# A hybrid decoder block on one core: the key's decay to its block's end from a backward scan

## The chip, the core and the metric

The kernel runs on one core of a Trainium2 chip. TensorE multiplies matrices, VectorE (DVE) and ScalarE (ACT) work element by element, GpSimd (POOL) does small side work, and SyncE (SP) issues nearly all DMA transfers. The metric is the device time of one execution in microseconds; the time before is the median of three runs. Each profile shows one execution.

## The reference

The input x has 1024 tokens of 1024 features, in float32. One layer computes

```python
proj = x @ w_in        # -> q, f, i, o_gate, pool_v, gate_a, gate_b
f = lb + (1 - lb) * sigmoid(f_pre);  k = 1 - f;  log_f = log(f)
# S_t = diag(f_t) S_{t-1} + k_t v_t^T,  o_t = S_t^T q_t,  for 8 heads of 128, in blocks of 16 tokens:
G = cumsum(log_f within a block);  G_last = its last value
q_dec = q * exp(G);  k_inv = k * exp(-G);  k_to_end = k * exp(G_last - G)
scores = causal(q_dec @ k_inv^T);  o = scores @ v + q_dec @ state
state = exp(G_last) * state + k_to_end^T @ v
a = (rmsnorm(o) * g * sigmoid(o_gate)) @ w_a
b = (causal_mean_w(pool_v) - pool_v) @ w_pool * pool_scale
x = LN(alpha * x + (sigmoid(gate_a) * a + sigmoid(gate_b) * b) @ w_out)
x = LN(alpha * x + relu(x @ w_up)^2 @ w_down)
```

Three quantities matter here. exp(G) is the product of the forget gates f from the start of a block up to and with a token. exp(-G) is its inverse. exp(G_last - G) is the product of the gates behind a token up to the block's end.

## The kernel before

Every large product is made in a form with seven block products in place of eight, and each operand is split into a high and a low part in a rounded format, so that one float32 product is three matmuls (lines 199 to 201: high by high, high by low, low by high; each 128 x 128 by 128 x 512). The split of a weight (lines 117 and 118) is a cast on ScalarE into `hi` and a subtraction on VectorE into `lo`. There are ten weight tiles (`NW`), so five pairs. `pair` makes two columns of blocks at a time; results leave PSUM by a copy on ScalarE (line 268) or a sum on VectorE (line 272), and functions called `take` do what follows (a sigmoid, for example).

The stages are: the values i (up to about 100 us of the profile); the stage of the recurrence, in which the projections for q, f, the output gate, the pools and the gates run between the recurrences of 8 heads in 2 halves of 512 tokens (about 120 to 560 us); the pooling products and the end of the gates (to about 650 us); w_a and w_out with the merge, the first layer norm, then w_up and w_down and the second layer norm (to the end).

`hgrn(h, u, ...)` is the recurrence of one head h in one half u. Features lie on the 128 partitions and tokens along the free axis. 512 tokens are 32 blocks of 16 (`NB`, `SUB`). Line 808 makes `fd`, the products of the gates from each block's start, with a scan over 256 tokens at a time: the state is at each step the larger of itself and an entry of `starts`, times the gate; `starts` is 1 at a block's first token and 0 elsewhere, and as all products are at most 1, the scan begins anew at each block. Line 810 on ScalarE turns the gates into k = 1 - f in place. Lines 812 to 814 invert all of `fd` (`r`, tile tC) in four pieces of 128. GpSimd copies the 32 block ends of `fd` into `T` (line 816) and makes the small products for 32 and 64 tokens, `p32`, `p64`, `eq`, `ek` and `dec`, from it (to line 835). VectorE multiplies q by `fd` (line 838), makes the key to its block's start, `kc = k * r` (line 840, tile tD), and the key to its block's end, `kr = kc * T` (line 842, tile tE).

The score is made over pairs of blocks of 16. For each pair there is a reference point in its middle: the end of the even block. The keys of an even block are taken at its end (line 843 copies them from `kr` over `kc` on ScalarE), and the queries of an even block are divided by the block's whole decay (line 846, with `r` at the block's last token). The keys of an odd block stay at its start, and so do its queries (line 845). Then lines 850 to 862 carry queries and keys on to the ends of 32, 64 and 128 tokens, up to `ke` (line 862, tile tC again), which is transposed on TensorE and makes the new state (lines 865 to 880). Lines 883 to 905 make the scores, lines 908 to 930 the output, its norm and its product with the output gate (line 929), which SyncE stores (line 930).

All tiles come from pools with rings of buffers (`RINGS`): tC has two before. A tile that is asked for again waits until its earlier use is over. The order of instructions on each engine is fixed when the program is built: a planner simulates the program with its own costs and puts each engine's instructions in the order in which they come up; `tc.high_priority` and `tc.issue_after` move some of them. So a change in one place can move instructions of other parts. Each engine runs its queue strictly in order. The last recurrence (head 7, second half) has a high priority (line 949), and its outputs are read back by `o_sums` (line 602) for the product with w_a.

Of the kernel before, what the change touches and what calls it, by code (L numbers as in the profile page):

```python
# [9 lines left out]
F32 = mybir.dt.float32  # L10
# [3 lines left out]
ALU = mybir.AluOpType  # L14

_TC = dict(schedule_with_timeline_sim=True)
P = 128
# [5 lines left out]
HALF = 512  # L23
CH = HALF // P
SUB = 16
NB = HALF // SUB
# [4 lines left out]
QUARTER = HALF // 2  # L31
# [11 lines left out]
def tile_hybrid_block(  # L43
# [19 lines left out]
    V, A, G, PE = nc.vector, nc.scalar, nc.gpsimd, nc.tensor  # L63
# [16 lines left out]
    def nm(s):  # L80
        seq[0] += 1
        return f"{s}_{seq[0]}"
# [63 lines left out]
    r = [None] * 8  # L146
# [252 lines left out]
    with tc.tile_pool(name="xr", bufs=8, side="right", reuse_waits="tile") as xr:  # L399
# [68 lines left out]
        def parts(rows):  # L468
            return [split(row, row_tile) for row in rows]
# [62 lines left out]
        w = parts(b11)  # L532
        first_tokens("a12", "tr")
        onto_chain(w, "a11", True, copied(c11, c_late))
        with behind_parts("a11"):
            w = parts(b21)
        second_tokens("s3", "tr")
        by_rows(w, "a12", take_p2)
        with behind_parts("a12"):
            for k in range(CH):  # L540
                V.tensor_sub(b22[k], b22[k], b12[k])
            w = parts(b22)
# [3 lines left out]
        with behind_parts("s3"):  # L546
# [3 lines left out]
            w = parts(b21)  # L550
        second_tokens("s2")
        by_rows(w, "a22", take_p4)
        with behind_parts("a22"):
            w = parts(b22)
# [3 lines left out]
        with tc.issue_after(taken["a22", 1]):  # L558
            for k in range(CH):
                V.tensor_sub(b12[k], b12[k], b11[k])  # L560
            w = parts(b12)
# [7 lines left out]
        with behind_parts("s1"):  # L569
            w = parts(b22)  # L570
# [18 lines left out]
    def loaded(src, tile_of):  # L589
        t = tile_of()  # L590
        nc.sync.dma_start(out=t, in_=src)
        return t
# [20 lines left out]
    hgp = hg_scope.enter_context(tc.tile_pool(name="hgp", bufs=1, reuse_waits="tile"))  # L613
    mg_scope = ExitStack()
    with tc.tile_pool(name="tmp", bufs=1, side="right", reuse_waits="tile") as tmp:
        starts = hgp.tile([P, NB // 2, SUB], F32, name="starts")
        G.memset(starts, 0.0)
        G.memset(starts[:, :, 0:1], 1.0)
        att = [hgp.tile([P, CH, P], F32, name=f"att{i}") for i in range(1)]
        for t in att:  # L620
            G.memset(t, 0.0)
# [3 lines left out]
        sc = pp.tile([P, HALF], F32, tag="sc", name="sc", bufs=1)  # L625
        V.memset(sc, 0.0)

        RINGS = dict(q=3, f=3, og=2, v=2, tA=2, tC=2, st=2)

        def tt(tag, dtype=F32):  # L630
            pool = tmp if tag in ("q", "f", "og", "v") else hgp
            return pool.tile([P, HALF], dtype, tag=tag, name=nm(tag), bufs=RINGS.get(tag, 1))

        def small(tag, shape, bufs=2):
            n = math.prod(shape[1:])
            t = hgp.tile([P, max(n, LINE)], F32, tag=tag, name=nm(tag), bufs=bufs)[:, :n]
            return t if len(shape) == 2 else t.rearrange("p (a b) -> p a b", b=shape[2])
# [29 lines left out]
        def values(h, u):  # L667
            src = vd[u][h // CH].rearrange("p (c d) -> p c d", d=HALF)[:, :, h % CH * P : (h % CH + 1) * P]
            return loaded(src, lambda: tmp.tile([P, CH, P], F32, tag="v", name=nm("v"), bufs=RINGS["v"]))

# [120 lines left out]
        def blk(t):  # L791
            return t.rearrange("p (b s) -> p b s", s=SUB)

        def pairs_of(t):
            return t.rearrange("p (b e s) -> p b e s", e=2, s=SUB)
# [4 lines left out]
        def bc(a, shape):  # L800
            return a.unsqueeze(len(a.shape)).to_broadcast(shape)

        def hgrn(h, u, ft, q, v, og, state):

            fd = tt("tA")
            for i in range(2):
                w = slice(i * QUARTER, (i + 1) * QUARTER)
                V.tensor_tensor_scan(fd[:, w], starts.rearrange("p b s -> p (b s)"), ft[:, w], 1.0, ALU.max, ALU.mult)
            k = ft
            A.activation(k, ft, AF.Identity, bias=cmask[:, P - 1 : P], scale=-1.0)  # L810
            r = tt("tC")
            for i in range(CH):
                w = slice(i * P, (i + 1) * P)
                V.reciprocal(r[:, w], fd[:, w])  # L814
            T = small("T", [P, NB])
            G.tensor_copy(T, blk(fd)[:, :, SUB - 1])
            T2 = T.rearrange("p (b e) -> p b e", e=2)
# [18 lines left out]


            V.tensor_mul(q, q, fd)
            kc = tt("tD")
            V.tensor_mul(kc, k, r)  # L840
            kr = tt("tE")
            V.tensor_mul(blk(kr), blk(kc), bc(T, [P, NB, SUB]))
            A.copy(pairs_of(kc)[:, :, 0], pairs_of(kr)[:, :, 0])
            qc = tt("tF")
            A.copy(pairs_of(qc)[:, :, 1], pairs_of(q)[:, :, 1])
            V.tensor_mul(
                pairs_of(qc)[:, :, 0], pairs_of(q)[:, :, 0],
                bc(pairs_of(r)[:, :, 0, SUB - 1], [P, NB // 2, SUB]),
            )
            V.tensor_mul(pairs_of(q)[:, :, 1], pairs_of(q)[:, :, 1], bc(T2[:, :, 0], [P, NB // 2, SUB]))  # L850
            V.tensor_mul(pairs_of(kr)[:, :, 0], pairs_of(kr)[:, :, 0], bc(T2[:, :, 1], [P, NB // 2, SUB]))
# [21 lines left out]
            st = tt("st")  # L873
# [35 lines left out]
            for c in range(CH):  # L909
                w = slice(c * P, (c + 1) * P)  # L910
# [7 lines left out]
            for c in range(CH):  # L918
                w = slice(c * P, (c + 1) * P)
# [3 lines left out]
            for c in range(CH):  # L923
                w = slice(c * P, (c + 1) * P)
# [19 lines left out]
        for h in range(HEADS):  # L944
            fs, qs = nxt
            state = None
            for u in range(2):
                v, og = values(h, u), loaded(ogd[h][u], lambda: tt("og"))
                with tc.high_priority(PRIO_LAST) if (h, u) == (HEADS - 1, 1) else nullcontext():
                    state = hgrn(h, u, fs[u], qs[u], v, og, state)  # L950
                    if (h, u) == (HEADS - 1, 1):
                        tags = iter(("tD", "tE", "tF", "tC"))
                        o_sums(h - CH, lambda: tt(next(tags)))
                if h + 1 < HEADS and u:
                    nxt = head_inputs(h + 1)
                    if h % 2:
                        output_gates(h + 1)
                for what, j in EXTRAS.get((h, u), ()):
                    dict(gates=gates, pooled=pooled, pool_products=pool_products, o_sums=o_sums)[what](j)
# [439 lines left out]
```

## Time and profile before

| what | value |
|---|---|
| median of the runs | 1463.76 us (1461.53, 1463.76, 1465.18) |
| span of the profiled execution | 1462.4 us |
| TensorE busy | 1440.6 us, 99% |
| VectorE busy | 1140.0 us, 78% |
| ScalarE busy | 756.9 us, 52% |
| GpSimd busy | 63.5 us, 4% |
| DMA | 226.82 MB, 155 GB/s over the span |

The profiled execution's own time is known by its span, from the first to the last instruction; it lies 1.4 us under the median and within the spread of the runs. In the profile PE is TensorE's matmuls and PEld its weight loads, which overlap. Matmuls overlap one another: one of 512 columns is shown with 389 ns, while they start about 226 ns apart. A group's row gives the line, engine, operation, output and inputs, the count, then busy us, mean ns of one, and the engine's idle time just before with what ended it. Rows of stretches give busy time of PE, PEld, DVE, ACT and POOL with counts, then the granted TensorE clock, the DMA share and GB/s.

### The profile page before, as it was taken

To read this page: it belongs to the slowest core of one execution; us is meant where nothing else is said; L and a number is where in the kernel's file an instruction comes from. 1 tells how busy PE (TensorE), PEld (TensorE's weight loads), DVE (VectorE), ACT (ScalarE), POOL (GpSimd) and SP (SyncE) were. 2 spreads that over 40 slices of the span, in tenths; PEclk is the share of its full clock that TensorE was granted. 3 is DMA by queue.
4 is the path that set the end of the run, shared out by engine and by line. 5 is a ranking of instruction groups with operands and counts; after the bars stand their busy time and mean duration, and the time that the engine had idled before them with its cause. 6 is when DMAs were issued, how large, how long until landed. Compare 5 with 4: busy or idle time off the path is not lost.

```text
span 1462.4 us, 20665 instructions
## 1 busy us (share of the span) xinstructions
PE 1440.6 (99%) x7377; PEld 1187.2 (81%) x7377; DVE 1140.0 (78%) x1838; ACT 756.9 (52%) x1383; POOL 63.5 (4%) x244
## 2 busy tenths in 40 slices
PE   9999999999999999999999999999999999999997
PEld 7888888888888888777888878888888888888886
DVE  5968989899998695767985598666666787777977
ACT  5445565665656566455442366555555443333535
POOL 0002000001000020000002100000000100000000
PEclk9999999999999999999999999999999999999999
DMA  7232233223333537987563135445464874445422
GB/s 252 75 120 87 88 100 103 94 87 109 95 109 108 168 122 248 345 285 238 186 226 135 69 98 195 133 150 172 144 232 156 284 267 146 160 135 170 128 72 115
DMA packets 160615, 226.82 MB, mean 155 GB/s; under 512 B 11232, under 2 KB 84480, under 8 KB 160512
## 3 DMA queue, kind: packets, MB, share of 16 engines
q1 hardware_dynamic: 158576, 218.93, 45.1%
q0 software_dynamic: 1152, 4.19, 0.8%
q10 hardware_dynamic: 784, 2.38, 0.5%
q8 instruction: 58, 0.95, 0.3%
q14 instruction: 45, 0.37, 0.1%
HBM read 154.16 MB, written 71.30 MB: 154 GB/s over the span
## 4 chain that ended last, share of the span: by engine, by line
PE 87%; DVE 5%; DMA 4%; ACT 2%; issue 1%; SPq 0%; DVEq 0%; ACTq 0%
PE ps_pj L199 14%; PE ps_pj L200 14%; PE ps_pj L201 14%; PE ps_pj L1282 4%; PE ps_pj L1281 4%; PE ps_pj L1280 4%; PE ps_pj L104 2%; PE ps_pj L105 2%; PE ps_pj L106 2%; PE ps_tr L1282 1%; PE ps_tr L1281 1%; PE ps_tr L1280 1%; PE ps_hg L199 1%; PE ps_sc L199 1%; PE ps_hg L200 1%
## 5 line engine op out<-in xcount | busy, mean ns | idle before, releaser
L199 PE MATMUL ps_pj<-act,w 128*128 128x512 f32 x1068 | 419.9, 395 | 6.4 <-ACT w L117 2.0
L200 PE MATMUL ps_pj<-act,w 128*128 128x512 f32 x1068 | 417.3, 391 | 0.5 <-DVE act L123 0.5
L201 PE MATMUL ps_pj<-act,w 128*128 128x512 f32 x1068 | 411.8, 392 | 0.1
L199 PEld LDWEIGHTS ps_pj<-act,w 128*128 128x128 f32 x1068 | 200.3, 188 | 52.4 <-ACT w L117 3.9
L201 PEld LDWEIGHTS ps_pj<-act,w 128*128 128x128 f32 x1068 | 200.4, 188 | 42.9 <-DVE w L118 1.4
L200 PEld LDWEIGHTS ps_pj<-act,w 128*128 128x128 f32 x1068 | 200.6, 188 | 41.0 <-DVE act L123 0.9
L117 ACT CAST w<-t 128x512 fp32r<-128x512 f32 x170 | 104.7, 619 | 115.5 <-PE ps_pj L200 52.1
L118 DVE TENSOR_TENSOR w<-raw,w 128x512 fp32r<-128x512 f32 x143 | 99.3, 700 | 62.3 <-ACT w L117 48.4
L117 ACT CAST w<-raw 128x512 fp32r<-128x512 f32 x143 | 88.3, 620 | 96.1 <-PE ps_pj L200 45.4
L118 DVE TENSOR_TENSOR w<-t,w 128x512 fp32r<-128x512 f32 x170 | 116.4, 688 | 26.2 <-ACT w L117 23.3
L1242 ACT CAST act<-act 128x1024 fp32r<-128x1024 f32 x66 | 67.0, 1051 | 108.9 <-issue 35.0
L1282 PE MATMUL ps_pj<-act,act 128*128 128x512 f32 x240 | 93.0, 389 | 0.0
L1281 PE MATMUL ps_pj<-act,act 128*128 128x512 f32 x240 | 93.0, 389 | 0.0
L1243 DVE TENSOR_TENSOR act<-act,act 128x1024 fp32r<-128x1024 f32 x66 | 79.4, 1221 | 17.3 <-ACT act L1242 17.3
L1280 PE MATMUL ps_pj<-act,act 128*128 128x512 f32 x240 | 92.4, 389 | 0.0
L272 DVE TENSOR_TENSOR c<-c,ps_pj 128x512 f32<-128x512 f32 x95 | 64.7, 682 | 28.9 <-PE ps_pj L201 23.7
L268 ACT COPY c<-ps_pj 128x512 f32<-128x512 f32 x96 | 55.3, 584 | 11.3 <-PE ps_pj L201 10.4
L814 DVE RECIPROCAL tC<-tA 128x128 f32<-128x128 f32 x64 | 54.6, 910 | 0.0
L1281 PEld LDWEIGHTS ps_pj<-act,act 128*128 128x128 f32 x240 | 45.0, 188 | 9.4
L1280 PEld LDWEIGHTS ps_pj<-act,act 128*128 128x128 f32 x240 | 45.0, 188 | 9.3
L1282 PEld LDWEIGHTS ps_pj<-act,act 128*128 128x128 f32 x240 | 45.0, 188 | 9.3
L238 DVE TENSOR_TENSOR t<-raw,raw 128x512 f32<-128x512 f32 x43 | 29.6, 689 | 18.0 <-DMA raw<-in_w_in_dram 14.2
(415 smaller groups left out, 2728.3 us busy)
## 6 DMA issues: line engine op xcount, KB each, us to landing
h<-c SPq DMA_DIRECT2D x106, 256.0 KB, 2.4
act<-h SPq DMA_DIRECT2D x78, 256.0 KB, 3.0
raw<-in_w_in_dram SPq DMA_DIRECT2D x64, 256.0 KB, 3.4
draw<-in_w_down_dram SPq DMA_DIRECT2D x16, 1024.0 KB, 8.3
raw<-in_w_up_dram SPq DMA_DIRECT2D x30, 512.0 KB, 4.2
raw<-in_w_in_dram SPq DMA_DIRECT2D x18, 512.0 KB, 3.9
hf<-h SPq DMA_DIRECT2D x34, 256.0 KB, 3.0
c<-o SPq DMA_DIRECT2D x24, 256.0 KB, 3.8
```

The lines of the kernel that those rows point to most:

```text
L117: A.copy(hi, src)
L118: V.tensor_sub(lo, src, f(hi))
L199: PE.matmul(ps, wh[:, k], th, start=first and k == 0, stop=False, skip_group_check=True)
L200: PE.matmul(ps, wh[:, k], tl, start=False, stop=False, skip_group_check=True)
L201: PE.matmul(ps, wl[:, k], th, start=False, stop=k == CH - 1, skip_group_check=True)
L268: A.copy(t, ps)
L272: V.tensor_add(t, t, ps)
L1242: A.copy(hi, src)
L1243: V.tensor_sub(lo, src, f(hi))
L1280: PE.matmul(ps, hh[:, w], wh, start=fresh and n == 0, stop=False, skip_group_check=True)
L1281: PE.matmul(ps, hh[:, w], wl, start=False, stop=False, skip_group_check=True)
L1282: PE.matmul(ps, hl[:, w], wh, start=False, stop=n == M - 1, skip_group_check=True)
```

## The change

A second pair of scans on VectorE runs backward over the gates and writes into one fixed tile, `to_end`, for each token the product of the gates behind it up to its block's end. The key to its block's end is then `kr = k * to_end`. The inverse is taken of the 32 block ends only (`rT`). The key of an odd block at its start comes from `kr` times the inverse of its block's decay; that of an even block is copied from `kr` as before. `to_end`'s last column is set to 1 once, before the stage. The ring of tC falls from two buffers to one, as `r` is gone and only `ke` uses it. In the changed kernel the backward scans stand at lines 813 and 817, k = 1 - f at line 821, the small reciprocal at 823, `kr` at 850, the odd part of `kc` at 853 and `ke` at 872; from there on lines are ten higher than before.

```diff
+        first_of = starts.rearrange("p b s -> p (b s)")
+        to_end = hgp.tile([P, HALF], F32, name="to_end")
+        G.memset(to_end[:, HALF - 1 :], 1.0)
...
-        RINGS = dict(q=3, f=3, og=2, v=2, tA=2, tC=2, st=2)
+        RINGS = dict(q=3, f=3, og=2, v=2, tA=2, st=2)
...
-                V.tensor_tensor_scan(fd[:, w], starts.rearrange("p b s -> p (b s)"), ft[:, w], 1.0, ALU.max, ALU.mult)
+                V.tensor_tensor_scan(fd[:, w], first_of, ft[:, w], 1.0, ALU.max, ALU.mult)
+
+            V.tensor_tensor_scan(
+                to_end[:, HALF - 2 : QUARTER - 1 : -1], ft[:, HALF - 1 : QUARTER : -1], first_of[:, 1:],
+                1.0, ALU.mult, ALU.max,
+            )
+            V.tensor_tensor_scan(
+                to_end[:, QUARTER - 1 :: -1], ft[:, QUARTER : 0 : -1], first_of, 0.0, ALU.mult, ALU.max,
+            )
             k = ft
             A.activation(k, ft, AF.Identity, bias=cmask[:, P - 1 : P], scale=-1.0)
-            r = tt("tC")
-            for i in range(CH):
-                w = slice(i * P, (i + 1) * P)
-                V.reciprocal(r[:, w], fd[:, w])
+            rT = small("rT", [P, NB])
+            V.reciprocal(rT, blk(fd)[:, :, SUB - 1])
+            rT2 = rT.rearrange("p (b e) -> p b e", e=2)
...
             V.tensor_mul(q, q, fd)
+            kr = tt("tE")
+            V.tensor_mul(kr, k, to_end)
             kc = tt("tD")
-            V.tensor_mul(kc, k, r)
-            kr = tt("tE")
-            V.tensor_mul(blk(kr), blk(kc), bc(T, [P, NB, SUB]))
             A.copy(pairs_of(kc)[:, :, 0], pairs_of(kr)[:, :, 0])
+            V.tensor_mul(pairs_of(kc)[:, :, 1], pairs_of(kr)[:, :, 1], bc(rT2[:, :, 1], [P, NB // 2, SUB]))
...
-                bc(pairs_of(r)[:, :, 0, SUB - 1], [P, NB // 2, SUB]),
+                bc(rT2[:, :, 0], [P, NB // 2, SUB]),
```

## The prediction

> **What bounds the kernel now.** I read the page's head first, then busy time by stage, then what PE waits for, then the VectorE groups of the recurrence. The head, with the chain that ended last:
>
> ```profile
> span 1462.4 us, 20665 instructions
> ...
> PE 1440.6 (99%) x7377; PEld 1187.2 (81%) x7377; DVE 1140.0 (78%) x1838; ACT 756.9 (52%) x1383; POOL 63.5 (4%) x244
> ...
> PE 87%; DVE 5%; DMA 4%; ACT 2%; issue 1%; SPq 0%; DVEq 0%; ACTq 0%
> ```
>
> TensorE is busy for 99% of the span and makes 87% of the chain; VectorE makes 5%. The change takes nothing from TensorE, so it can only win time in which TensorE stands still. How much that is, by stage (the recurrence runs from about 120 to 560 us, with its last outputs at 582 us; the columns are each engine's busy us, then the granted clock, the DMA share and GB/s):
>
> ```profile
> 0.00:120.00 120.00, 116.77 (x543) 97.23 (x544) 82.84 (x140) 59.05 (x102) 2.79 (x34) 1.00 0.42 143
> 120.00:560.00 440.00, 437.26 (x2907) 360.17 (x2906) 391.47 (x764) 266.04 (x596) 41.88 (x196) 1.00 0.35 110
> 560.00:640.00 80.00, 78.04 (x355) 63.82 (x354) 51.02 (x83) 39.63 (x77) 0.00 (x0) 1.00 0.91 305
> 640.00:700.00 60.00, 56.46 (x236) 44.82 (x235) 47.28 (x76) 33.62 (x62) 0.00 (x0) 0.97 0.76 260
> 700.00:1462.40 762.40, 752.03 (x3344) 621.12 (x3342) 567.42 (x777) 358.54 (x548) 18.85 (x14) 1.00 0.47 159
> ```
>
> In the recurrence VectorE is busy 391.47 of 440 us (89%), by far its densest stage, yet TensorE idles there for only 440 - 437.26 = 2.74 us. Then come 80 - 78.04 = 1.96 us up to 640, and 60 - 56.46 = 3.54 us up to 700, where DMA is at 0.76 to 0.91 and VectorE has room. The waits of TensorE, for 120 to 560 us and then for 560 to 700 us (us in total, times, longest):
>
> ```profile
> PE ps_pj L199 <- ACT w L117: 1.2, 1, 1.2
> PE ps_pj L199 <- ACT c L268: 1.1, 2, 0.7
> PE ps_pj L199 <- DVE c L272: 0.4, 1, 0.4
> ```
>
> ```profile
> PE ps_pj L199 <- ACT act L122: 1.6, 1, 1.6
> PE ps_pj L104 <- ACT w L117: 1.4, 1, 1.4
> PE ps_pj L199 <- ACT w L117: 0.8, 1, 0.8
> PE ps_pj L199 <- ACT f L724: 0.6, 1, 0.6
> ```
>
> The longer of the two 1.1 us waits shows how a reciprocal reaches TensorE. The VectorE timeline, then ACT's and PE's at the same place (start, us, instruction, idle before it):
>
> ```profile
> 399.42 2.56 DVE L814 RECIPROCAL tC<-tA 128x128 f32<-128x128 f32 x3
> ...
> 402.07 0.94 DVE L814 RECIPROCAL tC<-tA 128x128 f32<-128x128 f32 x1
> 402.94 0.62 DVE L838 TENSOR_TENSOR q<-q,tA 128x512 f32<-128x512 f32 x1
> ...
> 404.23 0.68 DVE L272 TENSOR_TENSOR c<-c,ps_pj 128x512 f32<-128x512 f32 x1
> ```
>
> ```profile
> 404.94 0.63 ACT L693 ACTIVATE c<-c 128x512 f32<-128x512 f32 x1 [0.94 <-DVE c L272]
> 405.48 1.06 ACT L268 COPY c<-ps_pj 128x512 f32<-128x512 f32 x2
> ```
>
> ```profile
> 406.10 0.50 PE L199 MATMUL ps_pj<-act,w 128*128 128x512 f32 x1 [0.72 <-ACT c L268]
> ```
>
> Four reciprocals delay the sum L272, ScalarE stands before L693, its copy of the next bank is late, and TensorE stops for 0.72 us.
>
> **The change part by part.** The VectorE groups (count, busy us, mean ns, idle before):
>
> ```profile
> L118 DVE TENSOR_TENSOR w<-t,w 128x512 fp32r<-128x512 f32 x76 | 52.1, 689 | 10.1 <-ACT w L117 8.9 <-PE ps_pj L200 1.0
> L814 DVE RECIPROCAL tC<-tA 128x128 f32<-128x128 f32 x64 | 54.6, 910 | 0.0
> L808 DVE TENSOR_TENSOR_SCAN tA<-starts,f 128x256 f32<-128x256 f32 x32 | 20.3, 676 | 2.7 <-ACT f L651 1.6 <-PE ps_hg L915 1.1
> L842 DVE TENSOR_TENSOR tE<-tD,T 128x512 f32<-128x512 f32 x16 | 11.0, 687 | 0.0
> L840 DVE TENSOR_TENSOR tD<-f,tC 128x512 f32<-128x512 f32 x16 | 11.0, 686 | 0.0
> L851 DVE TENSOR_TENSOR tE<-tE,T 128x256 f32<-128x256 f32 x16 | 6.8, 422 | 0.0
> L922 DVE RECIPROCAL ss<-ss 128x4 f32<-128x4 f32 x16 | 2.6, 163 | 5.7 <-ACT ss L921 5.7
> ```
>
> Removed, 16 times (8 heads, 2 halves): four 128-wide reciprocals and two full products. By the groups: 54.6 + 11.0 + 11.0 = 76.6 us of VectorE.
>
> Added, 16 times: two backward scans of 255 and 256, a reciprocal of 32 strided elements, one full product (kr = k * to_end, like L840) and one half product (the odd blocks of kc, like L851). The scans are priced by the forward ones: 20.3 us. No row shows a scan with a step of -1; its bounds are the forward 676 ns and twice that, and I take the lower, the same operation over the same number of elements. The small reciprocal lies between 163 ns (4 wide) and 910 ns (128 wide): 163 + 28 * (910 - 163)/124 = 332 ns, 5.3 us in all. With 11.0 and 6.8 us the sum is 43.4. At twice the scan's price it is 63.7, still a saving. VectorE therefore gets 76.6 - 43.4 = 33 us (bounds 13 to 33) back of 391, about 2.1 us per half.
>
> The rows give a reciprocal (910 - 163)/124 = 6.0 ns per element. [...]
>
> What of 33 us reaches the end? TensorE's order has the same 6743 rows in both programs, and from the last pooling products, at about 600 us, all queues issue in the same order. Before that the planner moves the recurrence forward: the last turned output stands behind 2058 of the 512-wide matmuls instead of 2092, at 100 us per 442 (row below) 7.7 us earlier. In VectorE's queue, priced by these rows, the longest stretch between two weight splits (L118) falls from 11.5 to 7.9 us, and stretches over 5 us from 26 to 13.
>
> Term A: the waits for L268 and L272 in the recurrence, 1.1 + 0.4 us, whose cause is VectorE's lateness, go: -1.5. The 1.2 us on L117 stays: ScalarE, with a table load, is late there.
>
> Term B: the wait of 1.4 us on L117 at 599 us, to which the chain leads from the last output's multiplication by its gate through stores and loads, goes, since that output is 7.7 us ahead: -1.4. Its bounds are 0 (the load of pooling weights ahead of it is as late as before) and -1.96 (all idle time of that stage).
>
> Added waits. k = 1 - f overwrites f, so ScalarE's L821 waits for four scans instead of two, up to 2 * 0.676 = 1.35 us more, and behind it on ScalarE stand casts of weights (L117) and evictions (L268). Bounds: 0, and 16 * 1.35 = 21.6 us if all of it reached TensorE every time. I take 0: ten weight tiles are five high-and-low pairs, and a pair feeds 12 matmuls, 2.7 us, so the lead ahead of TensorE is several times the delay; the same planner also sets L821 a place in the queue by when it expects the scans. Single buffers: tC (ke alone) drops from two to one, to_end is one tile. Two of the 16 products that write ke now wait for TensorE's transposes of the half before (none did); behind them VectorE's splits are queued. Bounds 0 and about 2 us each; I take 0, covered by the 2.1 us gained per half. TensorE, the DMAs and SP's queue get no instruction; GpSimd one 1-wide memset before the stage, while it waits anyway.
>
> Sum: -1.5 - 1.4 = -2.9. Against the profiled execution that is 1462.4 - 2.9 = 1459.5 of span; its span stands 1.4 us under the runs' median of 1463.76, so the median should come to 1460.9, say 1461.
>
> **The rivals.**
>
> First, the gain goes deeper. All 2.74 + 1.96 us of idle time up to 640 us goes, and half of the 3.54 us up to 700, since the o loads come earlier. That stage also ran at a lower clock, right after TensorE had stood still:
>
> ```profile
> 684.05 1.01 PE L199 MATMUL ps_pj<-act,w 128*128 128x512 f32 x2 [1.56 <-ACT act L122]
> ```
>
> ```profile
> 686.40:689.80 3.40, 3.40 (x10) 2.66 (x9) 3.40 (x7) 1.16 (x3) 0.00 (x0) 0.50 1.00 334
> ```
>
> A clock of 0.50 for 3.40 us costs 1.7 us; without the 1.56 us stop it may go. 4.7 + 1.8 + 1.7 = 8.2 us: 1455.6. For it: the outputs come 7.7 us earlier. Against it: that stage's queue order is unchanged and its waits are for loads. [...]
>
> Second, no effect: VectorE's lateness was never what TensorE paid for, term A is replaced by other waits of like size and B is held by a DMA: 1463.8. For it: 89% busy and only 2.74 us idle. A busy matmul is not proof of full speed, so I compare with a stage in which VectorE is at 63%:
>
> ```profile
> 900.00:1000.00 100.00, 100.00 (x442) 82.59 (x441) 63.45 (x97) 56.11 (x96) 0.00 (x0) 1.00 0.47 153
> ```
>
> [...]
>
> Third, the other side: L821 behind four scans holds ScalarE's casts. Place: L117 behind L821. It decides from where the 1.35 us is more than the lead in finished weight pairs, as at the 1.2 us wait, where L810 stood right ahead of the cast. If half of the 16 halves pay: 8 * 1.35 = 10.8 us, less the 2.9, is +7.9: 1471.7. Against it: VectorE's stretches get shorter.
>
> **How the numbers follow.** 0.3% is 4.4 us, about what a measurement of this kernel can tell from no change. Forecast 0.48 (its own range 1458 to 1465), deeper gain 0.25, no effect 0.14, ScalarE held 0.13. Faster than 1459.4: 0.22 of the deeper gain and 0.10 of the forecast's lower part, 0.32. Slower than 1468.2: 0.11. The rest is 0.57. The range reaches from 1455, the deeper gain, to 1468, where the third rival pays for four or five halves.
>
> **What would show it.** Right: no L814; new scans at about 676 ns; VectorE near 360 us in 120 to 560; no TensorE wait on L268 or L272 there; the stop at 599 gone. Wrong: TensorE waits on L117 with L821 ahead of it on ScalarE, scans far over 676 ns, or a stop in 640 to 700 that grows and halves the clock again.

## The result, and the profile after

The changed kernel takes 1470.9 us (median of 4 runs, 1469.33 to 1471.83) against 1462.9 us for the kernel before on the same chip: a ratio of 1.0045, 95% interval 1.0033 to 1.0058. It is slower by 0.45%, a small difference but one clear of its interval, where 1461 and "no change" were forecast. Runs of one program scatter by about 3 us to either side, so each time of a kernel below is a median.

The head of the page after, with the chain that ended last:

```profile
span 1469.4 us, 20680 instructions
...
PE 1444.3 (98%) x7377; PEld 1189.0 (81%) x7377; DVE 1112.0 (76%) x1822; ACT 756.1 (51%) x1383; POOL 90.7 (6%) x245
...
PE 83%; DVE 6%; DMA 4%; ACT 4%; issue 2%; SPq 0%; DVEq 0%; ACTq 0%
```

Busy time by stage after (columns as before):

```profile
0.00:120.00 120.00, 116.56 (x541) 97.07 (x542) 82.83 (x140) 59.06 (x102) 2.82 (x35) 1.00 0.42 143
120.00:560.00 440.00, 435.81 (x2895) 358.75 (x2894) 362.20 (x747) 263.58 (x594) 69.07 (x196) 1.00 0.34 109
560.00:640.00 80.00, 75.67 (x333) 60.82 (x332) 46.76 (x75) 35.76 (x70) 0.00 (x0) 0.98 0.85 281
640.00:700.00 60.00, 57.36 (x242) 45.65 (x241) 46.40 (x74) 33.48 (x60) 0.00 (x0) 0.97 0.73 248
```

VectorE does in the recurrence what was priced: 391.47 to 362.20 us, 29.3 less. TensorE gets nothing of it. Its idle time there grows from 2.74 to 440 - 435.81 = 4.19 us, and from 560 to 640 us from 1.96 to 4.33 us, at a granted clock of 0.98. What it waits for, in 120 to 560 us and then in 560 to 700 us (us in total, times, longest):

```profile
PE ps_pj L199 <- ACT c L268: 2.0, 3, 1.0
PE ps_pj L199 <- ACT w L117: 1.2, 2, 1.0
PE sc L894 <- DVE tE L861: 0.6, 1, 0.6
```

```profile
PE ps_pj L199 <- ACT c L268: 2.2, 1, 2.2
PE ps_pj L199 <- ACT w L117: 1.8, 1, 1.8
PE ps_pj L105 <- DVE w L118: 1.2, 1, 1.2
PE ps_pj L199 <- DVE c L272: 0.6, 1, 0.6
```

The new groups on VectorE (count, busy us, mean ns, idle before):

```profile
L850 DVE TENSOR_TENSOR tE<-f,to_end 128x512 f32<-128x512 f32 x16 | 11.0, 689 | 1.1 <-ACT f L821 0.9 <-PE sc L894 0.2
L813 DVE TENSOR_TENSOR_SCAN to_end<-f,starts 128x255 f32<-128x255 f32 x16 | 10.8, 672 | 0.0
L817 DVE TENSOR_TENSOR_SCAN to_end<-f,starts 128x256 f32<-128x256 f32 x16 | 10.7, 666 | 0.0
L853 DVE TENSOR_TENSOR tD<-tE,rT 128x256 f32<-128x256 f32 x16 | 6.7, 416 | 0.0
L823 DVE RECIPROCAL rT<-tA 128x32 f32<-128x32 f32 x16 | 5.5, 343 | 0.0
```

The three late stops, in the timeline after (start, us, instruction, idle before it):

```profile
581.62 0.69 DVE L238 TENSOR_TENSOR t<-raw,raw 128x512 f32<-128x512 f32 x1 [3.01 <-DMA raw<-in_w_in_dram]
...
582.83 0.69 DVE L118 TENSOR_TENSOR w<-v,w 128x512 fp32r<-128x512 f32 x1
...
583.57 0.50 PE L105 MATMUL ps_pj<-w,q 128*128 128x512 f32 x1 [1.20 <-DVE w L118]
...
586.74 0.69 DVE L605 TENSOR_TENSOR tC<-tE,tC 128x512 f32<-128x512 f32 x1 [1.88 <-DMA tC<-o]
...
587.35 0.68 DVE L272 TENSOR_TENSOR c<-c,ps_pj 128x512 f32<-128x512 f32 x1
...
588.09 0.50 PE L199 MATMUL ps_pj<-act,w 128*128 128x512 f32 x1 [0.56 <-DVE c L272]
```

```profile
600.86 0.62 ACT L117 CAST q<-raw 128x512 fp32r<-128x512 f32 x1 [4.62 <-DMA raw<-in_w_pool_dram]
...
603.55 0.59 ACT L268 COPY c<-ps_pj 128x512 f32<-128x512 f32 x1 [1.04 <-DMA s<-c]
```

```profile
604.19 0.50 PE L199 MATMUL ps_pj<-act,w 128*128 128x512 f32 x1 [2.20 <-ACT c L268]
```

Each time a step that waits for a transfer stands at the head of VectorE's or ScalarE's queue, and behind it the split or eviction that TensorE needs next. After the last of them the clock is halved for 3.4 us; the second row is the same again at 666 us, behind another stop of 1.84 us:

```profile
604.60:608.00 3.40, 3.40 (x10) 2.63 (x9) 0.95 (x2) 1.14 (x2) 0.00 (x0) 0.50 1.06 405
666.00:669.40 3.40, 3.40 (x9) 2.45 (x8) 2.22 (x4) 1.56 (x4) 0.00 (x0) 0.50 0.36 112
```

To place the loss I use one mark for all kernels: when the n-th of the 5856 matmuls of 512 columns (the wide ones) starts, worked out from the matmuls' starts in each trace (us). How many small matmuls stand between them differs a little with the order.

| kernel | 1900th | 2200th | between | 5800th |
|---|---|---|---|---|
| before | 526.3 | 606.8 | 80.5 | 1440.2 |
| after | 529.4 | 614.8 | 85.4 | 1447.3 |

Of the 7.1 us at the 5800th, 3.1 are there at the 1900th, 4.9 come in the next 300, and 0.9 is won back behind them. The 3.1 us are in part no loss: by its 1900th wide matmul the changed kernel has started 1328 small ones, the kernel before 1286.

Two cautions for what follows. Each run was timed beside the kernel before on its own chip, where that kernel's median lay between 1462.9 and 1464.9 us; runs of different chips are compared by their ratios. And marks, waits and stops come from one profiled execution of each kernel, which can lie some us off its median (e1's 3.5 us above, f2's 1.9 below). In the ten traces that share the changed kernel's order up to the 1900th wide matmul, that matmul starts between 529.3 and 531.7 us.

### The profile page after: what moved, and what is told of

Same layout as the page of the kernel before. It is cut to its first block, busy times and chain, and to the rows that moved or that the text cites. A ratio compares the mean times of both kernels' runs of the same rounds, so it can differ in the third digit from the quotient of the medians.

```text
span 1469.4 us, 20680 instructions
## 1 busy us (share of the span) xinstructions
PE 1444.3 (98%) x7377; PEld 1189.0 (81%) x7377; DVE 1112.0 (76%) x1822; ACT 756.1 (51%) x1383; POOL 90.7 (6%) x245
## 3 DMA queue, kind: packets, MB, share of 16 engines
q0 software_dynamic: 1152, 4.19, 0.8%
## 4 chain that ended last, share of the span: by engine, by line
PE 83%; DVE 6%; DMA 4%; ACT 4%; issue 2%; SPq 0%; DVEq 0%; ACTq 0%
PE ps_pj L199 14%; PE ps_pj L200 13%; PE ps_pj L201 13%; PE ps_pj L1290 4%; PE ps_pj L1292 4%; PE ps_pj L1291 4%; PE ps_pj L104 2%; PE ps_pj L105 2%; PE ps_pj L106 2%; PE ps_tr L1290 1%; PE ps_tr L1292 1%; PE ps_tr L1291 1%; DMA c<-o 1%; PE ps_sc L199 1%; PE ps_hg L199 1%
## 5 line engine op out<-in xcount | busy, mean ns | idle before, releaser
L117 ACT CAST w<-t 128x512 fp32r<-128x512 f32 x170 | 105.1, 620 | 135.5 <-PE ps_pj L200 77.4
L118 DVE TENSOR_TENSOR w<-raw,w 128x512 fp32r<-128x512 f32 x143 | 99.5, 699 | 63.2 <-ACT w L117 47.5
L118 DVE TENSOR_TENSOR w<-t,w 128x512 fp32r<-128x512 f32 x170 | 116.1, 686 | 27.2 <-ACT w L117 25.0
L117 ACT CAST w<-raw 128x512 fp32r<-128x512 f32 x143 | 88.4, 621 | 83.2 <-PE ps_pj L200 41.3
L272 DVE TENSOR_TENSOR c<-c,ps_pj 128x512 f32<-128x512 f32 x95 | 64.7, 681 | 33.4 <-PE ps_pj L201 28.9
L268 ACT COPY c<-ps_pj 128x512 f32<-128x512 f32 x96 | 55.3, 586 | 7.5 <-PE ps_pj L201 6.4
L238 DVE TENSOR_TENSOR t<-raw,raw 128x512 f32<-128x512 f32 x43 | 29.6, 689 | 21.7 <-DMA raw<-in_w_in_dram 17.9
L1155 ACT ACTIVATE c<-c 128x512 f32<-128x512 f32 x46 | 29.1, 633 | 21.5 <-DVE c L272 21.5
```

The source lines that it names most:

```text
L117: A.copy(hi, src)
L118: V.tensor_sub(lo, src, f(hi))
L268: A.copy(t, ps)
L272: V.tensor_add(t, t, ps)
```

## The experiments

**Is it VectorE's load, the place of the backward scans, or the order as such?** In the trace after, the two backward scans of a head's second half often stand on VectorE between kr (L850) and its carry (L861) of the first half; ScalarE's copy L866 then waits for L861 (13.1 us in 10 waits, against 5.1 in 6 for the same step before), and evictions stand behind it. First theory: this costs the time. Rivals: something in VectorE's load; or only that the planner makes another order.

e1: the changed kernel, backward scans issued behind the previous half's ke product.

```diff
+            with tc.issue_after(done_ke[0]) if done_ke else nullcontext():
                 V.tensor_tensor_scan(to_end[...], ...)   # both
...
+            done_ke[:] = [V.tensor_mul(b32(ke), b32(kr), ...).ins]
```

> The changed kernel, but the backward scans of a half are queued on VectorE behind the product that writes ke of the half before; nothing else differs. Theory A (the scans of the second half, which stand between kr and its carry L861 in all 8 heads, delay what ScalarE and TensorE wait for): the 3.1 us by which the changed kernel is behind at the end of the recurrence shrink to under 1, no TensorE stop behind the score matmuls (0.6 to 1.2 us at 171, 221, 409 and 528 us) is left, and the time falls from 1470.9 by 2 to 4 us, to 1467 to 1469, as the 4 us lost after 560 us have another cause. Theory B (every new order scatters by some us): the recurrence may lose anything from 0 to 4 us. Theory C (the scans or their effect on GpSimd slow the stage wherever they stand): 3 us are still lost by 560 us, 1471.

Measured: 1467.5 us, ratio 1.0023 (1.0012 to 1.0033). The total lies where the first theory put it, but its reason does not hold. The 1900th wide matmul was to come earlier by over 2 us; it starts at 531.3 us against after's 529.4, and even without the 2.0 us by which this execution stood still longer at 7 us, ahead of the recurrence, it would only be level with it. Stops of 0.5 to 1.7 us are still there at 171, 225, 411 and 530 us, and the largest is another, TensorE waiting 3.0 us from 581 us on for ScalarE's scaling of a head's outputs.

e2: the kernel before with copies in place of the reciprocals; it leaves the inverse out.

```diff
-                V.reciprocal(r[:, w], fd[:, w])
+                V.tensor_copy(r[:, w], fd[:, w])
```

> The kernel before with each of the 64 reciprocals of 128 replaced by a copy of the same tile (the inverse is left out, so the output is not the reference's). VectorE gets some 45 us back and no scan is added. If less VectorE work helps and the loss of the change is in its scans (A, C): 1459 to 1462, all stops of TensorE on L268 and L272 in the recurrence gone. If a lighter VectorE, by moving the recurrence forward in the order, is itself what costs (B or the late stage): 1464 to 1471, lost after 560 us.

e3: the kernel before, two reciprocals of 256 columns instead of four of 128.

```diff
-            for i in range(CH):
-                w = slice(i * P, (i + 1) * P)
+            for i in range(2):
+                w = slice(i * QUARTER, (i + 1) * QUARTER)
```

> The kernel before with two reciprocals of 256 in place of four of 128: the same arithmetic, some 3 us less of VectorE in all. By A and C it stays within 2 us of 1462.9. By B, a reordering alone scatters: it may differ by 3 us or more in either direction although the work is the same.

e5: the changed kernel with four unused reciprocals a half.

```diff
+            ke = tt("tC")
+            for i in range(CH):
+                w = slice(i * P, (i + 1) * P)
+                V.reciprocal(ke[:, w], fd[:, w])
```

> The changed kernel plus the four reciprocals of 128 that it saved, written to ke's tile before ke is and never read: VectorE carries 55 us more than in the changed kernel, and in the queue the second half's backward scans still stand ahead of L861 in all 8 heads. By A: the recurrence loses 4 to 8 us against the kernel before, 1472 to 1477. If the lighter VectorE and the earlier outputs were the cause of the late loss: that goes back to the 2 to 3 us of the kernel before, and the total is 1466 to 1470.

Measured: e2 1461.8 (0.9990, 0.9981 to 1.0000), e3 1465.4 (1.0015, 1.0003 to 1.0027), e5 1467.3 (1.0024, 1.0015 to 1.0033). VectorE in the recurrence, e2 and then e5:

```profile
120.00:560.00 440.00, 438.53 (x2907) 361.51 (x2906) 357.76 (x767) 264.47 (x596) 70.77 (x196) 1.00 0.34 109
```

```profile
120.00:560.00 440.00, 435.80 (x2878) 357.90 (x2878) 405.59 (x808) 257.37 (x579) 64.52 (x196) 1.00 0.34 108
```

34 us less of VectorE is worth about 0.1%; the changed kernel with 43 us more of it is not slower than without. e5 falls in the range of its second theory, but not by that theory's way: its stretch from the 1900th to the 2200th wide matmul still takes 84.0 us. e3 moves hardly any work and costs 1.4 us. This speaks against VectorE's load and for the order that the planner makes, without separating order and scans; the next runs hold one and change the other.

**Arithmetic and order apart.** At the end of tracing every engine's instructions are chained in a given order (an edge for the order of issue, no wait):

```diff
         tile_hybrid_block(tc, *args)
+        in_given_order(tc)
...
+    for nos in orders:                # one list of instructions per engine
+        for a, b in zip(nos, nos[1:]):
+            tc.add_manual_dep(by_no[b], by_no[a].name, NoSync, reason="order")
```

f1 and f2 are the changed kernel in the earlier kernel's order; they differ only in the backward scans, which stay behind the forward ones in f1 and may run ahead in f2. f3 is the earlier kernel in the changed one's order; its four reciprocals, for which that order has no place, stand at the first place they can behind a given step.

> The changed kernel's arithmetic with the earlier kernel's queue order: on TensorE, ScalarE, GpSimd, SyncE and VectorE every instruction that both kernels have stands where it stood before; the two backward scans of a half stand right behind its two forward scans, the small reciprocal in the place of the fourth reciprocal, the products of kr and kc in the places of kc and kr. Theory 'order' (the loss is what the planner's other order does, above all between 560 and 700 us): as the kernel before or a little under it, 1459 to 1465, and the first 512-wide lag at the end below 2 us. Theory 'arithmetic' (the backward scans in VectorE's queue hold ScalarE and TensorE wherever the rest stands): 1467 to 1473. Theory 'scans run ahead' (the cost comes from backward scans queued in front of the carry of the half before): as the kernel before, since here they stand behind that carry.

> As the run before it, but the backward scans may stand anywhere on VectorE: the planner puts those of a second half up to 30 instructions ahead of the forward scans of that half, right behind the kr product of the half before and in front of its carry, as in the changed kernel. Theory 'order': 1459 to 1465, the same as with the scans in place. Theory 'scans run ahead': 2 to 5 us above the run with the scans in place. Theory 'arithmetic': 1467 to 1473.

> The earlier kernel's arithmetic (four reciprocals of 128 columns, no backward scan) with the changed kernel's queue order of everything that both have. Theory 'order': 1467 to 1473, as the changed kernel, with stops of TensorE near 580 and 600 us. Theory 'arithmetic': 1460 to 1465. Theory 'scans run ahead': 1460 to 1466, since there are no scans to run ahead.

Measured: f1 1465.7 (1.0010, 1.000 to 1.002), f2 1462.8 (0.9995, 0.9986 to 1.0004), f3 1512.4 (1.0330, 1.0314 to 1.0346). In f2 the new arithmetic in the old order is as fast as the old kernel: there it costs nothing and wins nothing. "Arithmetic" falls, and "scans run ahead" with it, since f2, whose scans run ahead, is the faster of the two, by 2.8 us on the same chip; f1 came out just above the range of "order". f1's 1900th wide matmul starts at 529.4 us, f2's at 526.3. f1's largest stop in the recurrence shows what the scans do when they stay (its timeline on ScalarE, then TensorE):

```profile
193.04 0.72 ACT L821 ACTIVATE f<-f,cmask 128x512 f32<-128x512 f32 x1 [0.61 <-DVE to_end L817]
193.67 0.60 ACT L117 CAST w<-raw 128x512 fp32r<-128x512 f32 x1
```

```profile
194.32 0.50 PE L199 MATMUL ps_pj<-act,w 128*128 128x512 f32 x1 [1.95 <-ACT w L117]
```

This is the prediction's third rival at work: L821 behind four scans, a weight cast behind it. The kernel before and f2 stop for 1.23 us at the same place, so the scans add 0.7 us here. f3 went far beyond every expectation. Its recurrence:

```profile
120.00:560.00 440.00, 417.60 (x2630) 340.68 (x2629) 365.31 (x706) 240.85 (x546) 36.29 (x186) 0.97 0.31 95
```

TensorE idles 22.4 us there, and ScalarE's copy L843 waits 38.2 us for L842, which stands behind the reciprocals, against 6.0 us in the kernel before. My reading, which f3 alone supports: the new order has brought forward what the shorter arithmetic allows, and is unusable for the longer one, so VectorE's gain was real and was spent on an earlier place for the recurrence's steps. f3 does not tell what the order costs by itself, as its arithmetic does not fit it.

n1 tried the same with the order that the planner made for e2:

> The changed kernel's arithmetic in the queue order that the planner made for the run with copies in place of the reciprocals (that run: 1461.8), backward scans free. If the order sets the time: 1460 to 1463, below both kernels. If it is the arithmetic: 1466 or more.

Measured: 1473.1 (1.0061, 1.0046 to 1.0076), a miss: by the words of the expectation this is the range of "arithmetic". The 1900th wide matmul starts at 536.9 us against e2's 527.1. An order that suits copies does not suit backward scans, though VectorE is busy for nearly the same time between 120 and 560 us (359.4 and 357.8): L821 waits, in n1, for

```profile
ACT f L821 <- DVE to_end L817: 10.6, 7, 3.4
ACT f L821 <- DVE tA L811: 7.1, 6, 3.1
```

together 17.7 us, where e2's wait of the same step is 7.4 us; that these waits are what reaches TensorE was not followed. So "costs nothing" holds of the new arithmetic in f2's order, not in every order: an order has to fit its arithmetic.

**Where in the order.** h1, m1 and m2 are the changed kernel in its own order up to the 1900th, 2000th and 2100th wide matmul and in f2's order behind it; h2 is the reverse of h1.

```diff
-order of an engine: after's
+order of an engine: after's instructions before the cut, then the rest as f2 has them
```

> The changed kernel with its own queue order on all engines for its first 1900 matmuls 512 wide (to about 529 us) and the earlier kernel's order for all that follows. Theory 'late stage' (the order behind 530 us makes SyncE's loads late there and costs the 4 us seen between 560 and 610 us): 1462 to 1466. Theory 'recurrence' (the loss is made in the first 530 us, what follows only keeps it): 1467 to 1471. A third: the loss of 560 to 610 us comes from how the recurrence left the queues, so the order behind 530 us does not matter; then also 1467 to 1471, but with stops near 580 and 600 us.

> The reverse: the changed kernel's arithmetic, the earlier kernel's queue order (backward scans free, 1462.8 as a whole) for the first 1900 matmuls 512 wide, the changed kernel's own order behind them. Theory 'late stage': 1467 to 1471, with the stops near 580 and 600 us. Theory 'recurrence': 1461 to 1464.

> The changed kernel, its own queue order for its first 2000 matmuls 512 wide (to about 559 us; SyncE's 210 first transfers, up to but without the store o<-og of the last head's first half), the earlier kernel's order behind. With the cut at 1900 it was 1464.3; with no cut 1470.9. Theory 'store ahead' (that store, queued ahead of the next loads of w_in and w_pool, where it waited 5.5 us for its last product, makes them late): 1463 to 1466. Theory 'last head early' (the last head's recurrence steps, queued ahead of the projections' evictions on ScalarE and VectorE between 1900 and 2000, are what costs): 1467 to 1471.

> As before with the cut behind 2100 matmuls 512 wide (about 587 us; the store of the first half and SyncE's 236 first transfers are then in the changed kernel's order, the w_pool load and the two w_a loads of 595 us are not). Theory 'store ahead': 1466 to 1469, with the stops near 580 us and without that of 601 us. Theory 'pool load late' (the w_pool load of 595 us, followed at once by two w_a loads, is what stops TensorE at 601 us): 1466 to 1469 as well if both cost, 1463 to 1465 if only the later one does, 1469 to 1472 if only the earlier ones do.

| kernel | median, us | ratio to before (95%) | 1900th | 2200th | between | 5800th |
|---|---|---|---|---|---|---|
| h1, cut at 1900 | 1464.3 | 1.0001 (0.9991, 1.0011) | 530.3 | 608.4 | 78.1 | 1440.4 |
| m1, cut at 2000 | 1467.1 | 1.0027 (1.0015, 1.0039) | 529.6 | 609.9 | 80.3 | 1442.2 |
| m2, cut at 2100 | 1468.7 | 1.0033 (1.0021, 1.0045) | 531.0 | 614.4 | 83.4 | 1444.8 |
| after, no cut | 1470.9 | 1.0045 (1.0033, 1.0058) | 529.4 | 614.8 | 85.4 | 1447.3 |
| h2, reverse at 1900 | 1473.8 | 1.0062 (1.0041, 1.0083) | 527.6 | 618.2 | 90.6 | 1449.5 |
| f2, earlier order | 1462.8 | 0.9995 (0.9986, 1.0004) | 526.3 | 606.6 | 80.3 | 1437.1 |

"Late stage" holds. After's order of the first 1900 costs nothing in the end: h1 is late there, as after is, but has 42 more small matmuls behind it and makes the time good. With each later cut the ratio grows; neighbours from m1 on overlap in their intervals, the first and the last are far apart. The theories on single steps are not settled by this: m1 lies just inside "last head early" and above "store ahead", while m2, with stops of 1.1, 0.9 and 1.6 us at 579, 585 and 590 us and none at 601, fits "store ahead". h2 has 2.5 us of stops at its seam (528 and 530 us) that neither whole order has, with 3.4 us of half clock behind them; its further stops, at 586, 590 and 608 us, come 3 to 6 us behind after's three. TensorE in one stretch, after and then h1:

```profile
530.00:615.00 85.00, 80.57 (x429) 64.88 (x429) 54.32 (x96) 41.86 (x89) 4.42 (x10) 0.98 0.75 247
```

```profile
530.00:615.00 85.00, 84.24 (x457) 69.60 (x458) 57.90 (x103) 44.41 (x94) 4.93 (x10) 1.00 0.77 251
```

**Which instruction.** The stops suggest single steps: a store on SyncE that waited 5.0 us in front of two w_in loads (k4), two w_a loads beside the w_pool load (k5), both (k6), VectorE's L605 and L238 in front of L272 and L118 (k7), ScalarE's L117 in front of L268, and the last head's L930 in front of another L268 (k8; L879 stayed ahead of it), all seven moves (k9). Each run is after's order but for these places:

```diff
 k4, k6, k9  SyncE:   -ga<-c (L699), raw<-w_in x2        +raw<-w_in x2, ga<-c
 k5, k6, k9  SyncE:   -raw<-w_a x2, ... raw<-w_in x4     +... raw<-w_in x4, raw<-w_a x2
 k7, k9      VectorE: -L605, L272 ; L238 x2, L118        +L272, L605 ; L118, L238 x2
 k8, k9      ScalarE: -L117 q<-raw, ... L268 ; L930 x4, L268
                      +L268, L117 q<-raw, ... ; L268, L930 x4
```

> The changed kernel in its own queue order, but for one transfer on SyncE: the store ga<-c that waited 5.0 us for ScalarE's eviction until 576.7 us stands behind the two loads raw<-in_w_in that were queued after it and issued at 577.2 and 577.6 us. Theory 'SyncE' (a store that waits at the queue's head makes the next w_in loads late, and VectorE's split of them stops TensorE at 582 and 587 us, 2.1 us of excess): 1467.5 to 1469.5 against the changed kernel's 1470.9, and the stops at 582 and 587 us gone or below 0.5 us. Theory 'ScalarE and VectorE' (the last head's steps queued ahead of the evictions and splits set it; SyncE's order alone changes nothing): 1470 to 1472, stops as they were.

> The changed kernel in its own queue order, but for two transfers on SyncE: the two 512 KB loads raw<-in_w_a of 596.7 and 598.7 us stand behind the four w_in loads that follow. Theory 'SyncE' (they share the DMA engines with the w_pool load of 595.5 us, for which ScalarE waits 4.6 us with the eviction behind it): w_pool's wait falls to about 2 us, the stop of 2.36 us at 601.6 us goes, and with it its stretch of half clock (3.4 us at half speed, 1.7 us): 1466.5 to 1469. Theory 'ScalarE and VectorE': 1470 to 1472.

> Both moves. Theory 'SyncE': 1463 to 1467, near the 1464.3 that the earlier kernel's order of this stage gave. Theory 'ScalarE and VectorE': 1470 to 1472.

> The changed kernel in its own queue order, but for two steps of VectorE: L605 (tC<-tE, which waited 1.88 us at 586.7 us for its transfer) stands behind the addition L272 that it kept from freeing a PSUM bank, and the split L118 of v stands in front of the two differences L238 that waited 3.01 us for their w_in load at 581.6 us. Theory 'VectorE' (a step that waits for a transfer at the head of VectorE's queue makes the stops at 582 and 587 us): those stops fall from 1.4 and 0.7 us to below 0.5, 1468.5 to 1470. Theory 'no single step' (the stage has so little room that the wait comes back at the next step): 1470 to 1472, other stops in their place.

> The changed kernel in its own queue order, but for two steps of ScalarE: the evictions L268 stand in front of what the earlier kernel had behind them, one ahead of the last head's L879 and L930, the other ahead of the cast L117 of w_pool, for which ScalarE waited 4.62 us until 600.9 us. Theory 'ScalarE' (that cast at the head of the queue makes the stop of 2.36 us at 601.6 us and its stretch of half clock): 1467 to 1469, stop below 1.2 us. Theory 'no single step' (the eviction then waits for its store s<-c, which ended 1.0 us of its wait already): 1470 to 1472.

> The moves of both and the two of SyncE (the store behind the w_in loads, the w_a loads behind the w_in loads) together, seven instructions in all. If these seven carry the loss of the stage: 1463 to 1467. If it lies in the order as a whole: 1468 to 1471.

Measured: k4 1471.8 (1.0048), k5 1469.6 (1.0034), k6 1469.3 (1.0036), k7 1472.4 (1.0057), k8 1479.3 (1.0103), k9 1476.1 (1.0084), intervals 0.001 to 0.002 to either side. None brings the time back; k5 and k6 lie within the interval of the changed kernel itself, and k8 and k9 came out slower than any expectation, k8 by 8 us against the changed kernel. "No single step" stands. What ScalarE waited for behind 560 us, in after, in k5 and in k8, says why:

```profile
ACT q L117 <- DMA raw<-in_w_pool_dram: 8.3, 2, 4.6
```

```profile
ACT q L117 <- DMA raw<-in_w_pool_dram: 9.4, 3, 4.7
```

```profile
ACT c L268 <- DMA s<-c: 8.2, 1, 8.2
ACT q L117 <- DMA raw<-in_w_pool_dram: 2.8, 1, 2.8
```

Without the w_a loads beside it the w_pool load is no faster: 5.4 us pass from its issue to the cast that waits for it, in k5 as in after. So sharing the DMA engines with those two loads was not the cause. With the eviction put first, it waits itself, 8.2 us, for the store that frees its tile. In k4 VectorE's wait for w_in falls to 1.5 us and TensorE stops 2.8 us for L272 instead. In these runs the wait moves to another step.

## Why the prediction was wrong

*What bounds the kernel, and the prices.* Right. Scans stepping backward cost 672 and 666 ns (676 taken), the small reciprocal 343 ns (332), the products 689 and 416. The saving of 33 us was measured as 29.3 between 120 and 560 us. That TensorE pays little for VectorE's load was right too: f2, with the new arithmetic in the old order, is within 0.15% of the kernel before.

*Term A, -1.5.* It did not come: in place of 1.1 + 0.4 us on L268 and L272 there are 2.0 us on L268 and 0.6 on L861. In the old order (f2) TensorE's waits on the two do fall to 0.2 and 0.3 us, but those on L117 grow from 1.2 to 1.7. The "no effect" rival described this, and it describes the arithmetic.

*Term B, -1.4, is the step that failed, with the term for the new order that was missing beside it.* Term B took the last output as 7.7 us earlier, from its place among the wide matmuls, and let the order's shift only win: its bounds were -1.96 and 0. SyncE's stores of the last head's output, before and then after:

```profile
561.51 0.32 SPq L930 DMA_DIRECT2D o<-og  x1
...
582.39 0.32 SPq L930 DMA_DIRECT2D o<-og  x1
```

```profile
560.01 0.34 SPq L940 DMA_DIRECT2D o<-og  x1
...
579.74 0.38 SPq L940 DMA_DIRECT2D o<-og  x1
```

They left 1.5 and 2.7 us earlier, since TensorE itself ran late: the place in the order was right (the last output's transposes stand behind 2058 wide matmuls instead of 2092), the time was not. The stop at 599 us went, and others came at 582, 587 and 602 us. Behind the 1900th wide matmul 67 instructions of ScalarE, 86 of SyncE, 90 of VectorE and 318 matmuls stand in another place than in h1's order, and with the recurrence's steps ahead, loads, evictions and splits come behind them. That had no row in the sum, and no bound above zero. It measured +4.9 us between the 1900th and the 2200th wide matmul, +7.3 against h1's order of the same work (the two rows from 530 to 615 us show 3.7 us of that as idle time of TensorE, and the half clock at 604.6 us is 1.7 more; the rest was not told apart), and 1.0045 against 1.0001 in the ratios.

*Added waits taken at 0.* Half right. L821's waits grew only from 4.8 to 9.2 us (6.1 on the scans, 3.1 on L811), because the planner ran the backward scans ahead. Where they stay behind the forward ones, as in f1, L821 waits 12.8 us for them, they hold ScalarE's casts, and the kernel is 2.8 us slower than f2: the mechanism that was taken at 0 is real there. The third rival's time, 1471.7, is close to the measured one by luck: what cost the time was something else, and with f2's order the rival's mechanism costs nothing that can be measured. The two single buffers did not show: VectorE has no idle time in front of L872, which writes `ke`, or of L813, which writes `to_end`.

*Chances and range.* The only case on the slower side was an added wait. That the planner's order could come out worse by itself was no case at all, though the change in order had been seen. e3, an edit almost without content, moved the time by 1.4 us, and the runs of the same arithmetic in other orders lie between 1462.8 and 1479.3 us: a range that ended at 1468 left this out.

*Open:* which of the queue positions between the 1900th and the 2200th wide matmul cost the time. The runs show that the order behind the 1900th carries the loss, and that seven single places picked from the stops do not carry it.

## What to carry to other kernels

Where a planner orders the queues, an edit that makes an engine cheaper also reorders every other one: compare the new queue orders stage by stage, and give the stage with the least slack (here the one with late loads and a DMA share of 0.85 to 0.91) a price of either sign. Two kinds of runs told the causes apart here: the new arithmetic in the old order, and the two orders joined at a chosen matmul. A saving on an engine that the bound engine hardly waits for can be worth nothing, as 29 us were here, and the instruction at the head of a stop is not yet its cause: moved alone, it handed the wait on.

## What the hardware showed that was not expected

Nine of GpSimd's ten small copies and products of the recurrence took longer in the changed kernel, though none was changed; the tenth, p<-p of 128x8, went from a mean of 707 ns to 401. The copy of T, before and then after:

```profile
L816 POOL COPY T<-tA 128x32 f32<-128x32 f32 x16 | 6.1, 379 | 212.7 <-DVE tA L808 202.2 <-DVE pA L746 10.5
```

```profile
L826 POOL COPY T<-tA 128x32 f32<-128x32 f32 x16 | 14.5, 904 | 223.1 <-DVE tA L811 223.1
```

All of GpSimd's work between 120 and 560 us grew from 41.88 to 69.07 us; with copies for the reciprocals (e2) it was 70.77, with the old reciprocals in the new order (f3) 36.29, and with reciprocals added to the changed kernel, but at another place (e5), 64.52. The time of the copy goes with what VectorE runs at that moment. Copy by copy, for 14 of the 16 in the trace after: 233 and 234 ns beside a reciprocal or a product with an input in PSUM (L939); 540 to 544 ns seven times with the first backward scan (L813) beside it, ending 110 ns behind the start of the second one (L817); 1.4 to 2.4 us five times beside a row of products, sums or differences with both inputs in SBUF, ending 170 to 180 ns behind the start of the instruction that follows the row. No run here was made to separate this from other causes. It cost next to nothing: in the stage, one step waited 0.2 us for GpSimd (L821, once).

Stops of TensorE of 2.20 and 1.84 us, from 602.0 and 663.7 us on, were each followed by 3.4 us at half clock, 1.7 us each; with h1's order this stage has neither. So with the half clock these two stops cost 3.9 and 3.5 us, nearly twice their length. It need not be so: f1's stop of 1.95 us that ended at 194.3 us was followed by the full clock. Nor does the order settle it. Ten traces have the same pair of stops, 0.6 and 0.96 us long, at about 170 us: in h1, m2, k5 and k8 3.4 us of half clock follow from 173 us on, in after, m1, k4, k6, k7 and k9 none. What decides it is not shown here; between these executions, which share one order up to there, it makes 1.7 us.
